# Attention beside a projection: TensorE in emission order, the scores and value products of two heads in turn in bursts, q, k and biases requested first

## The chip, the cores and the metric

The kernel runs on one core of a Trainium2 chip. The metric is the device time of one execution in microseconds, and lower is better. A core has a matrix engine (TensorE, PE in the profile; its weight loads are PEld), two engines for elementwise work (VectorE, DVE; ScalarE, ACT), GpSimd (POOL), and SyncE (SP), which in this kernel issues all DMA transfers from one queue. Each engine works through its own queue in order; semaphores tie the queues together.

## The reference

One layer over 512 tokens of width 1024. Branch A is a bidirectional Mamba-2 scan whose result `y` (2048 wide) goes through `w_proj_ssd`. Branch B is attention in three groups of 4 heads of width 64, with dilation 1, 4 and 16 and a window of half-width 64; the j-th heads of the three groups are combined by their softmax denominators.

```
for gi, (window, dilation) in enumerate(((128, 1), (512, 4), (2048, 16))):
    scores = einsum(q, k) / 8 - slope * dist          # window of |rel| <= 64 steps
    m = max(scores); p = exp(scores - m); den = sum(p)
    o = einsum(p, v) / den;  lse = m + log(den)
w = softmax(lse over the three groups);  y_att = sum(w * o) @ w_proj_attn
mix = (gate_a * (y_ssd @ w_proj_ssd) + gate_b * y_att) @ w_out
h = layer_norm(alpha * x + mix)
out = layer_norm(alpha * h + relu(h @ w_up)^2 @ w_down)
```

## The kernel before, in words

The stages follow each other on one TensorE: v and dt, the combined input projection interleaved with the scan (to 493.9 us), the attention interleaved with the first 12 of 16 pieces of the projection of `y` (`proj_a`, PSUM tiles `ps_pa`), then the last four pieces with the projection of the attention (`proj_b`, `ps_pb`), the output projection (`ps_o`), a layer norm, and the two MLP products.

The large products are float32 split in two halves of a reduced format (`mm3`, three matmuls a step, 512 columns each, lines 125 to 127). Each weight piece of 512 KB is loaded to `wraw` (line 87, three buffers), cast by ScalarE to `wh` (line 104) and subtracted by VectorE to `wl` (line 105), two buffers of each. A piece of `proj_a` is 24 matmuls.

The attention works on two heads at a time (`hh`), which lie in partitions 0 to 63 and 64 to 127 of the `q` and `k` tiles, so that a score matmul has 64 rows. In the trace each float32 matmul of the attention leaves two records. *Near* means dilation 1: scores at line 581 (192 or 256 columns), then VectorE adds the bias (589), takes the maximum (590) and negates it (592), and ScalarE takes the exponential (593). *Class* means dilations 4 and 16 (`gg`): scores at line 609, four matmuls of 128 columns a head, with lines 613 to 619 behind them. Then come the weights of the three groups (lines 624 to 641, tile `wg`); the near weights go through DRAM (`dr_w0`, lines 642 to 644) and back. `class_t` and `near_t` scale the probabilities and transpose them on TensorE (`ps_pt`, line 659; `ps_pn`, line 683), ScalarE copies them out, `class_v` (line 670, `ps_ac`) and `near_v` (line 698, `ps_an`) multiply by the values. A value product has 64 output partitions, the lower half for one head and the upper for the other, in one PSUM tile; near blocks b = 0 and b = 3 have one product of 64 rows and one of 128. `merge` adds near and class results and splits them into `ath` and `atl`, which `proj_b` reads.

`run` takes turns between the generators `attention()` and `proj_bg` by the amounts that they yield. In this stretch the order on every engine is then set by the scheduler of the program, which may move instructions ahead of others that wait; the same `run` around the scan stands in `tc.manual_schedule(engines={PE})`, which keeps TensorE in the order written. `ps_tile("tp", ..., 3)` and `ps_tile("y", ..., 2)` are PSUM tiles of one bank with 3 and 2 buffers. The pool `ap` holds the attention's tiles in memory that the scan's tiles had before (`reuse_waits`): a DMA into it waits until the old tile there has been read for the last time.

Of the kernel before, what the change touches and what calls it, by code (L numbers as in the profile page):

```python
# [10 lines left out]
F32 = mybir.dt.float32  # L11
# [5 lines left out]
P = 128  # L17
# [18 lines left out]
PACE = 0.6  # L36
# [8 lines left out]
def hybrid_layer_kernel(ctx: ExitStack, tc: tile.TileContext, t: dict, out: bass.AP):  # L45
# [504 lines left out]
    def attention():  # L550
        b0 = ap.tile([P, 4, 256], F32, name="b0")
        b12 = ap.tile([P, 8, P], F32, name="b12")
        dma.dma_start(b0, t["bias0"])
        dma.dma_start(b12, t["bias12"])
        v0 = ap.tile([P, 5, 256], F32, name="v0")
        vc = ap.tile([P, 4, 512], F32, name="vc")
        dma.dma_start(vc, dr_v.rearrange("(i r) d -> i r d", r=4)[:, :, 0:512])
        dma.dma_start(v0[:, 1:4, :], dr_v[64:448, 512:768].rearrange("(c p) d -> p c d", p=P))
        dma.dma_start(v0[0:64, 0, :], dr_v[0:64, 512:768])
        dma.dma_start(v0[0:64, 4, :], dr_v[448:512, 512:768])  # L560
# [6 lines left out]
        kr = [(max(0, P * b - 64), min(S, P * b + 192)) for b in range(NCH)]  # L567
        for i in range(2):
            qf = ap.tile([P, S], F32, name=f"q{i}", tag="q", bufs=2)
            kf = ap.tile([P, S], F32, name=f"k{i}", tag="k", bufs=2)  # L570
            dma.dma_start(qf, dr_qk[i])
            dma.dma_start(kf, dr_qk[6 + i])
            for bp in range(2):
                pss = [ps_tile("tp", f"ps_s0_{i}{bp}{hh}", 3) for hh in range(2)]
# [7 lines left out]
                for hh in range(2):  # L582
# [12 lines left out]
                    yield 2.0  # L595
        dma.dma_start(dr_st.rearrange("(b p) m -> p b m", p=P), st0.rearrange("p b a j -> p b (a j)"))
        for gg in range(2):
            for i in range(2):
                tl = 2 + gg * 2 + i
                qf = ap.tile([P, S], F32, name=f"q{tl}", tag="q", bufs=2)  # L600
                kf = ap.tile([P, S], F32, name=f"k{tl}", tag="k", bufs=2)
                dma.dma_start(qf, dr_qk[tl])
                dma.dma_start(kf, dr_qk[6 + tl])
                pss = [ps_tile("tp", f"ps_s{tl}_{hh}", 3) for hh in range(2)]
# [5 lines left out]
                for hh in range(2):  # L610
# [10 lines left out]
                    yield 2.0  # L621
# [23 lines left out]
        yield 1.0  # L645
# [3 lines left out]
        def tt_tile(name):  # L649
            nt[0] += 1  # L650
            return ap.tile([P, 4, P], F32, name=name, tag="qk"[nt[0] % 2], bufs=2)
# [12 lines left out]
        def class_v(i, hh, ptt):  # L664
            pr = slice(hh * HD, (hh + 1) * HD)
            if hh == 0:
                pcl[i] = ps_tile("y", f"ps_ac{i}", 2)
            for r in range(4):
                for gg in range(2):
                    pe.matmul(pcl[i][pr, r * P:(r + 1) * P], vc[:, r, (gg * 2 + i) * P + hh * HD:(gg * 2 + i) * P + (hh + 1) * HD], ptt[gg][:, r, :], start=(gg == 0), stop=(gg == 1))  # L670
# [20 lines left out]
        def near_v(i, b, tt):  # L691
            if b == 0:
                pn[i] = ps_tile("y", f"ps_an{i}", 2)
            for hh in range(2):
                pr = slice(hh * HD, (hh + 1) * HD)
                for q, (c0, c1, ck) in enumerate(cuts[b]):
                    n = c1 - c0
                    pe.matmul(pn[i][pr, b * P:(b + 1) * P], v0[:n, ck, (2 * i + hh) * HD:(2 * i + hh + 1) * HD], tt[:n, q * 2 + hh, :], start=(q == 0), stop=(q == 1))

        def merge(i):  # L700
            ac = ap.tile([P, S], F32, name=f"ac{i}", tag="vf", bufs=2)
# [5 lines left out]
        todo = []  # L707
        for i in range(2):
            for hh in range(2):
                a = class_t(i, hh, 0)  # L710
                yield 1.0
                b = class_t(i, hh, 1)
                yield 1.0
                for f in todo:
                    f()
                todo = [lambda i=i, hh=hh, a=a, b=b: class_v(i, hh, (a, b))]
# [298 lines left out]
```

## Time and profile before

| | |
|---|---|
| time, median of 3 runs (lowest, highest) | 1045.51 us (1044.17, 1045.84) |
| time of the profiled execution | 1044.5 us |
| its span, first to last instruction | 1042.7 us |
| TensorE busy | 1031.5 us, 99% |
| VectorE, ScalarE, GpSimd busy | 62%, 49%, 7% |
| first `ps_pa`, first `ps_pb` | 493.86 us, 608.3 us |
| output projection | 635.5 to 681 us |

Times inside the span are counted from the first instruction. A busy TensorE is one with a matmul in flight: since matmuls overlap, the step from one start to the next tells what one costs, and not its duration.

### The profile page before, as it was taken

Reading aid. Unit: us, or ns where it says so; the run is one execution under the profiler, and the core shown is the slowest. Engines: PE = TensorE matmul, PEld = TensorE weight load, DVE = VectorE, ACT = ScalarE, POOL = GpSimd, SP = SyncE. Lnnn points to the kernel's source line nnn. Section 1 sums busy time; section 2 is a strip of 40 time slices with the busy share of each in tenths; the row PEclk is TensorE's granted clock in tenths of the full one; section 3 lists DMA queues with packets and bytes.
Section 4 is the critical chain, followed back from the end, with each engine's and each line's share of the span. In section 5 each row is a group of like instructions: output and inputs, shape, how many; then the busy total and the mean of one; then the engine's idle time right before and its main releaser. Section 6 shows DMA issues by size and latency. Waiting matters only on the chain.

```text
span 1042.7 us, 13698 instructions
## 1 busy us (share of the span) xinstructions
PE 1031.5 (99%) x5169; PEld 852.9 (82%) x5169; DVE 648.6 (62%) x1009; ACT 511.6 (49%) x1009; POOL 74.1 (7%) x66
## 2 busy tenths in 40 slices
PE   9999999999999999999999999999999999999997
PEld 7888888888888888888777788798888888888886
DVE  4387988689979987784874356754442334443346
ACT  4444877478758865885564323213432113342120
POOL 0000101220221122021000000000000000000000
PEclk9999999999999999999999999999999999999999
DMA  6444354425543553655741358412333333333322
GB/s 233 153 156 126 130 186 159 141 92 177 187 132 118 186 185 118 201 183 172 253 124 51 111 154 292 129 41 59 88 97 101 101 94 91 99 102 101 89 93 80
DMA packets 48305, 140.42 MB, mean 135 GB/s; under 512 B 6512, under 2 KB 7280, under 8 KB 47984
## 3 DMA queue, kind: packets, MB, share of 16 engines
q1 hardware_dynamic: 48240, 139.56, 42.2%
q8 instruction: 40, 0.66, 0.3%
q14 instruction: 25, 0.20, 0.1%
HBM read 128.25 MB, written 11.30 MB: 134 GB/s over the span
## 4 chain that ended last, share of the span: by engine, by line
PE 94%; DVE 2%; DMA 1%; ACT 1%; issue 1%; POOL 0%; DVEq 0%; SPq 0%; ACTq 0%; POOLq 0%
PE ps_u L126 6%; PE ps_u L125 6%; PE ps_u L127 6%; PE ps_d L125 6%; PE ps_d L127 6%; PE ps_d L126 6%; PE ps_g L125 3%; PE ps_x L125 3%; PE ps_pa L125 3%; PE ps_g L127 3%; PE ps_g L126 3%; PE ps_x L126 3%; PE ps_x L127 3%; PE ps_pa L126 3%; PE ps_z L125 3%; PE ps_z L126 3%
## 5 line engine op out<-in xcount | busy, mean ns | idle before, releaser
L105 DVE TENSOR_TENSOR wl<-wraw,wh 128x1024 fp32r<-128x1024 f32 (+1 forms) x166 | 202.7, 1223 | 248.8 <-ACT wh L104 244.2
L104 ACT CAST wh<-wraw 128x1024 fp32r<-128x1024 f32 (+1 forms) x166 | 172.4, 1040 | 286.2 <-PE ps_d L127 108.6
L126 PE MATMUL ps_u<-htl,wh 128*128 128x512 f32 (+1 forms) x288 | 105.1, 366 | 0.3 <-DVE htl L857 0.3
L127 PE MATMUL ps_u<-hth,wl 128*128 128x512 f32 (+1 forms) x288 | 105.1, 365 | 0.0
L125 PE MATMUL ps_u<-hth,wh 128*128 128x512 f32 (+1 forms) x288 | 104.5, 366 | 0.3 <-ACT hth L856 0.2
L126 PE MATMUL ps_d<-wl,fh 128*128 128x512 f32 (+1 forms) x272 | 102.5, 377 | 0.0
L125 PE MATMUL ps_d<-wh,fh 128*128 128x512 f32 (+1 forms) x272 | 102.4, 377 | 0.0
L127 PE MATMUL ps_d<-wh,fl 128*128 128x512 f32 (+1 forms) x272 | 102.4, 377 | 0.0
L126 PEld LDWEIGHTS ps_u<-htl,wh 128*128 128x128 f32 x288 | 54.3, 189 | 9.3 <-DVE htl L857 0.5
L127 PEld LDWEIGHTS ps_u<-hth,wl 128*128 128x128 f32 x288 | 54.3, 189 | 8.8
L125 PEld LDWEIGHTS ps_u<-hth,wh 128*128 128x128 f32 x288 | 53.9, 188 | 9.3 <-ACT hth L856 0.7
L127 PEld LDWEIGHTS ps_d<-wh,fl 128*128 128x128 f32 x272 | 51.2, 188 | 9.5
L125 PEld LDWEIGHTS ps_d<-wh,fh 128*128 128x128 f32 x272 | 51.2, 188 | 9.4
L126 PEld LDWEIGHTS ps_d<-wl,fh 128*128 128x128 f32 x272 | 51.2, 188 | 9.4
L442 DVE SCALAR_TENSOR_TENSOR U<-bc,acr,U 128x128 f32<-128x128 f32 x128 | 47.5, 406 | 7.3 <-ACT U L440 7.1
L125 PE MATMUL ps_g<-xh,wh 128*128 128x512 f32 x128 | 51.5, 402 | 0.0
L125 PE MATMUL ps_pa<-yh,wh 128*128 128x512 f32 x128 | 51.0, 400 | 0.0
L125 PE MATMUL ps_z<-xh,wh 128*128 128x512 f32 x128 | 50.9, 398 | 0.0
L125 PE MATMUL ps_x<-xh,wh 128*128 128x512 f32 x128 | 50.9, 398 | 0.0
L126 PE MATMUL ps_pa<-yl,wh 128*128 128x512 f32 x128 | 50.5, 396 | 0.0
L127 PE MATMUL ps_pa<-yh,wl 128*128 128x512 f32 x128 | 50.0, 392 | 0.0
L127 PE MATMUL ps_x<-xh,wl 128*128 128x512 f32 x128 | 49.9, 390 | 0.0
(257 smaller groups left out, 2216.5 us busy)
## 6 DMA issues: line engine op xcount, KB each, us to landing
wraw<-in_w_in_dram SPq DMA_DIRECT2D x68, 512.0 KB, 3.6
bc<-dr_acr SPq DMA_DIRECT2D x32, 512.0 KB, 4.0
wraw<-in_w_up_dram SPq DMA_DIRECT2D x32, 512.0 KB, 3.6
wraw<-in_w_dn_dram SPq DMA_DIRECT2D x32, 512.0 KB, 3.6
be<-dr_ear SPq DMA_DIRECT2D x32, 256.0 KB, 4.4
wraw<-in_w_ps_dram SPq DMA_DIRECT2D x16, 512.0 KB, 3.9
dr_gate<-g SPq DMA_DIRECT2D x16, 256.0 KB, 2.0
wraw<-in_w_out_dram SPq DMA_DIRECT2D x8, 512.0 KB, 3.9
```

The lines of the kernel that those rows point to most:

```text
L104: act.copy(h[:, :width], r[:, :width])
L105: dve.tensor_sub(l[:, :width], r[:, :width], f32(h[:, :width]))
L125: pe.matmul(ps, lh, rh, start=(first and i == 0), stop=False)
L126: pe.matmul(ps, lh, rl, start=False, stop=False)
L127: ins = pe.matmul(ps, ll, rh, start=False, stop=(last and i == n - 1))
L442: dve.scalar_tensor_tensor(U[:, ch(c)], bcs[0][:, hh, ch(c)], acr[:, c, h:h + 1], U[:, ch(c)], op0=ALU.subtract, op1=ALU.min)
```

## The change

It has three parts. TensorE is kept in emission order around the `run` of attention and `proj_a`, and `proj_a` becomes a generator that yields after each 6 matmuls, so that the amounts yielded set where the attention's matmuls stand. The matmuls of the two heads stand in one burst in turn: near scores in four bursts, class scores in four, class value products in two, near value products with the head as the inner loop. And the queue's order changes: q and k of the first pair of heads, a bias and the next pair come first, the values after the near scores; the tiles for the values are allocated first, which moves the q, k and bias tiles to other addresses.

```diff
     def attention():
+        vc = ap.tile([P, 4, 512], F32, name="vc")
+        acs = [ap.tile([P, S], F32, name=f"ac{i}", tag="vf", bufs=2) for i in range(2)]
+        v0 = ap.tile([P, 5, 256], F32, name="v0")
+        load_qk(0)
         b0 = ap.tile([P, 4, 256], F32, name="b0")
+        dma.dma_start(b0, t["bias0"])
+        load_qk(1)
...
+        yield 4.0
+        def pair_tiles(n, name):
+            tag, bufs = (("tp", 3), ("y", 2))[n]
+            return [ps_tile(tag, f"{name}_{hh}", bufs) for hh in range(2)]
         for i in range(2):
             for bp in range(2):
-                pss = [ps_tile("tp", f"ps_s0_{i}{bp}{hh}", 3) for hh in range(2)]
+                pss = pair_tiles(bp, f"ps_s0_{i}{bp}")
...
-                    yield 2.0
+                yield 3.5
+        dma.dma_start(vc, dr_v.rearrange("(i r) d -> i r d", r=4)[:, :, 0:512])
...
-                    yield 2.0
+                yield 4.0
...
-        yield 1.0
+        yield 9.0
...
+        def class_v(i, ptt):
+            pcl[i] = ps_tile("y", f"ps_ac{i}", 2)
             for r in range(4):
                 for gg in range(2):
+                    for hh in range(2):
+                        v = vc[:, r, (gg * 2 + i) * P + hh * HD:(gg * 2 + i) * P + (hh + 1) * HD]
+                        pe.matmul(pcl[i][hh * HD:(hh + 1) * HD, r * P:(r + 1) * P], v, ptt[hh, gg][:, r, :], start=(gg == 0), stop=(gg == 1))
...
-            for hh in range(2):
-                for q, (c0, c1, ck) in enumerate(cuts[b]):
+            for q, (c0, c1, ck) in enumerate(cuts[b]):
+                for hh in range(2):
...
+        for k in range(0, 8, 2):
+            mm3(ps, [(wh[:, q * P:(q + 1) * P], wl[:, q * P:(q + 1) * P]) for q in (k, k + 1)], y_hl[i * 8 + k:i * 8 + k + 2], first=(i == 0 and k == 0), last=(i == 1 and k == 6))
+            if k < 6:
+                yield QT
...
-    run(attention(), proj_bg(a_order[:12]), 54.0, 62.4 * PACE)
+    with tc.manual_schedule(engines={mybir.EngineType.PE}):
+        run(attention(), proj_bg(a_order[:12]), 73.0, 48 * QT)
```

On TensorE, where the near scores begin (names before the arrow are the PSUM tile, behind it the operands; the last two digits of `ps_s0_000` are the block pair and the head). Before, from the last `ps_pa` ahead of the first score:

```order
L127 MATMUL ps_pa2_5039<-yh7_4775,wl78_4949 128x512
L581 MATMUL ps_s0_000_4853<-k0_4850,q0_4849 128x192
L581 MATMUL ps_s0_001_4854<-k0_4850,q0_4849 128x192
L581 MATMUL ps_s0_000_4853<-k0_4850,q0_4849 128x256
L581 MATMUL ps_s0_001_4854<-k0_4850,q0_4849 128x256
L581 MATMUL ps_s0_010_4920<-k0_4850,q0_4849 128x256
L581 MATMUL ps_s0_010_4920<-k0_4850,q0_4849 128x192
L125 MATMUL ps_pa3_4885<-yh8_4776,wh79_5035 128x512
L126 MATMUL ps_pa0_4885<-yl8_4808,wh79_5035 128x512
L127 MATMUL ps_pa0_4885<-yh8_4776,wl79_5036 128x512
L581 MATMUL ps_s0_011_4921<-k0_4850,q0_4849 128x256
L581 MATMUL ps_s0_011_4921<-k0_4850,q0_4849 128x192
```

Of the change, the second near burst with its neighbours:

```order
L124 MATMUL ps_pa1_4930<-yh1_4769,wh77_4869 128x512
L125 MATMUL ps_pa1_4930<-yl1_4787,wh77_4869 128x512
L126 MATMUL ps_pa1_4930<-yh1_4769,wl77_4870 128x512
L591 MATMUL ps_s0_01_0_4937<-k0_4842,q0_4841 128x256
L591 MATMUL ps_s0_01_1_4938<-k0_4842,q0_4841 128x256
L591 MATMUL ps_s0_01_0_4937<-k0_4842,q0_4841 128x192
L591 MATMUL ps_s0_01_1_4938<-k0_4842,q0_4841 128x192
L124 MATMUL ps_pa1_4930<-yh2_4770,wh77_4869 128x512
L125 MATMUL ps_pa1_4930<-yl2_4790,wh77_4869 128x512
L126 MATMUL ps_pa1_4930<-yh2_4770,wl77_4870 128x512
```

Before, the first score has 72 `ps_pa` matmuls ahead of it and only the first four scores change heads from one to the next; the rest stand in six small bursts with three `ps_pa` between them, one head in each after the first. Of the change, the first score has 18 `ps_pa` ahead of it, every burst holds two heads in turn, and 12 or 18 `ps_pa` stand between bursts; 54 stand between the last class scores and the first transpose.

On TensorE, the class value products of the first pair of heads (`tt0_0` is the transposed tile of `gg` 0 and head 0). Before, the end of the first head's burst, the near transposes and the start of the second head's:

```order
L670 MATMUL ps_ac0_5306<-tt0_0_5280,vc_4840 64x128
L670 MATMUL ps_ac0_5306<-tt1_0_5288,vc_4840 64x128
L683 MATMUL ps_pn0_0_5317<-tri_63,pt0_00_4859 64x128
L683 MATMUL ps_pn0_0_5317<-tri_63,pt0_00_4859 128x128
L683 MATMUL ps_pn0_0_5317<-tri_63,pt0_10_4910 64x128
L683 MATMUL ps_pn0_0_5317<-tri_63,pt0_10_4910 128x128
L670 MATMUL ps_ac0_5306<-tt0_1_5296,vc_4840 64x128
L670 MATMUL ps_ac0_5306<-tt1_1_5304,vc_4840 64x128
L670 MATMUL ps_ac0_5306<-tt0_1_5296,vc_4840 64x128
L670 MATMUL ps_ac0_5306<-tt1_1_5304,vc_4840 64x128
```

Of the change, the start of the one burst for both heads, with the `ps_pa` ahead of it:

```order
L124 MATMUL ps_pa4_5423<-yh3_4771,wh84_5344 128x512
L125 MATMUL ps_pa4_5423<-yl3_4793,wh84_5344 128x512
L126 MATMUL ps_pa4_5423<-yh3_4771,wl84_5345 128x512
L682 MATMUL ps_ac0_5436<-tt0_0_5360,vc_4837 64x128
L682 MATMUL ps_ac0_5436<-tt0_1_5388,vc_4837 64x128
L682 MATMUL ps_ac0_5436<-tt1_0_5374,vc_4837 64x128
L682 MATMUL ps_ac0_5436<-tt1_1_5405,vc_4837 64x128
L682 MATMUL ps_ac0_5436<-tt0_0_5360,vc_4837 64x128
```

The two bursts of eight matmuls, one a head, have become one of sixteen in which the head changes with every matmul, and the transposes that stood between them now follow it.

On SyncE, the requests from the last weight piece of this stretch before the attention's (`wraw80` is that piece). Before:

```order
L87 DMA wraw80_4946<-in_w_ps_dram 128x1024
L553 DMA b0_4835<-in_bias0_dram 128x1024
L554 DMA b12_4836<-in_bias12_dram 128x1024
L557 DMA vc_4840<-dr_v_72 128x4x512
L558 DMA v0_4839<-dr_v_72 128x3x256
L559 DMA v0_4839<-dr_v_72 64x256
L560 DMA v0_4839<-dr_v_72 64x256
L571 DMA q0_4849<-dr_qk_71 128x512
L572 DMA k0_4850<-dr_qk_71 128x512
L571 DMA q1_4977<-dr_qk_71 128x512
```

Of the change:

```order
L86 DMA wraw80_4924<-in_w_ps_dram 128x1024
L558 DMA q0_4841<-dr_qk_71 128x512
L559 DMA k0_4842<-dr_qk_71 128x512
L563 DMA b0_4845<-in_bias0_dram 128x1024
L558 DMA q1_4847<-dr_qk_71 128x512
L559 DMA k1_4848<-dr_qk_71 128x512
L566 DMA b12_4851<-in_bias12_dram 128x1024
L606 DMA vc_4837<-dr_v_72 128x4x512
L86 DMA wraw81_5007<-in_w_ps_dram 128x1024
L607 DMA v0_4840<-dr_v_72 128x3x256
L608 DMA v0_4840<-dr_v_72 64x256
```

The requests of `q0` and `k0` stood behind both biases and the four transfers of values, and now stand right behind `wraw80`; the values come behind the second bias, with a weight piece among them.

## Rows read from the trace of the kernel before

**Rows 1.** The page's opening: busy time of each engine with its share and instructions, TensorE's granted clock in 40 slices (tenths), and the chain that ended last by engine.

```profile
PE 1031.5 (99%) x5169; PEld 852.9 (82%) x5169; DVE 648.6 (62%) x1009; ACT 511.6 (49%) x1009; POOL 74.1 (7%) x66
...
PEclk9999999999999999999999999999999999999999
...
PE 94%; DVE 2%; DMA 1%; ACT 1%; issue 1%; POOL 0%; DVEq 0%; SPq 0%; ACTq 0%; POOLq 0%
```

**Rows 2.** Busy time in two stretches of 10 us of the attention: the stretch, its length, busy us and instructions of PE, PEld, DVE, ACT, POOL, the granted clock, the DMA engines' share and GB/s.

```profile
500.00:510.00 10.00, 10.00 (x46) 8.28 (x45) 7.21 (x10) 2.63 (x3) 0.00 (x0) 1.00 1.05 388
510.00:520.00 10.00, 9.85 (x45) 6.18 (x43) 8.42 (x34) 5.92 (x20) 0.00 (x0) 1.00 0.54 179
```

**Rows 3.** Three groups of the attention's matmuls by line and shape between 478 and 640 us: line, tiles, shape, count, busy us and mean ns of one (overlapped durations, not steps).

```profile
L609 PE MATMUL ps_s<-k,q 64*128 64x128 f32 x64 | 9.2, 285 | 0.0
L670 PE MATMUL ps_ac<-tt,vc 128*64 128x128 f32 x64 | 7.8, 276 | 0.0
L698 PE MATMUL ps_an<-tn,v 64*64 64x128 f32 x16 | 3.4, 294 | 0.0
```

**Rows 4.** TensorE in order of time in an undisturbed stretch of `ps_pa`: start, duration, line, tiles (first and last of 21 rows, one matmul each).

```profile
544.67 0.39 PE L125 MATMUL ps_pa<-yh,wh 128*128 128x512 f32 x1
...
549.20 0.39 PE L127 MATMUL ps_pa<-yh,wl 128*128 128x512 f32 x1
```

**Rows 5.** The score records alone in two stretches that split the first near burst (columns as in rows 2, without ACT and POOL; a count takes in records still running from before). The `ps_pa` behind the burst starts at the end of the second.

```profile
510.60:511.48 0.88, 0.86 (x8) 0.81 (x9) 0.00 (x0) 1.00 1.00 410
511.48:512.33 0.85, 0.85 (x6) 0.56 (x3) 0.00 (x0) 1.00 0.37 135
```

**Rows 6.** TensorE in order of time around the first class burst (4 matmuls of one head, 8 records).

```profile
522.37 0.40 PE L127 MATMUL ps_pa<-yh,wl 128*128 128x512 f32 x1
522.70 1.16 PE L609 MATMUL ps_s<-k,q 64*128 64x128 f32 x8
524.12 0.40 PE L126 MATMUL ps_pa<-yl,wh 128*128 128x512 f32 x1
```

**Rows 7.** TensorE in order of time in the value products of the first pair of heads, from two answers: a class burst of one head, the near block b = 0, and the block b = 1.

```profile
551.74 1.96 PE L670 MATMUL ps_ac<-tt,vc 128*64 128x128 f32 x16
553.63 0.63 PE L683 MATMUL ps_pn<-tri,pt 128*64 128x128 f32 x4
...
556.67 1.51 PE L698 MATMUL ps_an<-tn,v 64*64 64x128 f32 x8
558.11 0.33 PE L683 MATMUL ps_pn<-tri,pt 128*128 128x128 f32 x1
...
558.81 0.67 PE L698 MATMUL ps_an<-tn,v 128*64 128x128 f32 x8
559.40 0.52 PE L683 MATMUL ps_pn<-tri,pt 128*64 128x128 f32 x3
```

**Rows 8.** The DMA queue of SyncE in order of time, the nineteenth `ps_pa` on TensorE, DMA issues with KB each and median us to landing (of 496.5 to 503.3 us), and the time to landing of all loads of q and k.

```profile
496.56 0.33 SPq L87 DMA_DIRECT2D wraw<-in_w_ps_dram  x1
496.98 0.38 SPq L553 DMA_DIRECT2D b<-in_bias_dram  x1
...
500.59 0.61 SPq L571 DMA_DIRECT2D q<-dr_qk  x1
...
498.25 0.40 PE L127 MATMUL ps_pa<-yh,wl 128*128 128x512 f32 x1
...
b<-in_bias_dram SPq DMA_DIRECT2D x2, 512.0 KB, 5.1
...
wraw<-in_w_ps_dram SPq DMA_DIRECT2D x1, 512.0 KB, 3.7
...
DMA to landing us min/median/max: 2.6/3.3/8.0
```

**Rows 9.** VectorE in order of time over two blocks of near scores (line 589 add, 590 maximum).

```profile
520.48 0.41 DVE L589 TENSOR_TENSOR pt<-ps_s,b 128x256 f32<-128x256 f32 x1
...
520.87 0.34 DVE L589 TENSOR_TENSOR pt<-ps_s,b 128x192 f32<-128x192 f32 x1
521.13 0.66 DVE L590 TENSOR_REDUCE st<-pt 128x1 f32<-128x256 f32 x2
```

**Rows 10.** VectorE behind the last class scores (in brackets the idle time before and what ended it), and the first transpose of scaled probabilities on TensorE.

```profile
538.03 0.69 DVE L613 TENSOR_TENSOR pt<-ps_s,b 128x512 f32<-128x512 f32 x1 [1.60 <-PE ps_s L609]
...
545.55 0.69 DVE L738 SCALAR_TENSOR_TENSOR mixa<-ga,ps_pa 128x512 f32<-128x512 f32 x1 [2.88 <-PE ps_pa L127]
...
547.41 1.22 DVE L105 TENSOR_TENSOR wl<-wraw,wh 128x1024 fp32r<-128x1024 f32 x1
...
549.43 1.18 PE L659 MATMUL ps_pt<-tri,pt 128*128 128x128 f32 x8
```

**Rows 11.** Who waited for whom between 493 and 640 us: total us, times, longest.

```profile
DVE mixa L738 <- PE ps_pa L127: 16.1, 4, 8.5
```

**Rows 12.** TensorE's two longest waits in the output projection (in brackets the wait and what ended it).

```profile
652.22 0.51 PE L125 MATMUL ps_o<-wh,mixh 128*128 128x512 f32 x1 [0.23 <-ACT wh L104]
653.48 0.50 PE L126 MATMUL ps_o<-wl,mixh 128*128 128x512 f32 x1 [0.76 <-DVE wl L105]
```

**Rows 13.** The mean granted clock of the span (1 is full speed), and TensorE's longest wait of the whole execution, at its start.

```profile
core 0: 1042.7 us, clock 0.998
...
PE ps_warm L179 <- DVE warm L176: 1.2, 1, 1.2
```

More of the change, by code (lines that the diff above doesn't have):

```diff
@@ L550, in attention, with load_qk @@
     def attention():
+        vc = ap.tile([P, 4, 512], F32, name="vc")
+        acs = [ap.tile([P, S], F32, name=f"ac{i}", tag="vf", bufs=2) for i in range(2)]
+        v0 = ap.tile([P, 5, 256], F32, name="v0")
+        qk = {}
+        def load_qk(n):
+            qk[n] = [ap.tile([P, S], F32, name=f"{x}{n}", tag=x, bufs=2) for x in "qk"]
+            dma.dma_start(qk[n][0], dr_qk[n])
+            dma.dma_start(qk[n][1], dr_qk[6 + n])
+        load_qk(0)
         b0 = ap.tile([P, 4, 256], F32, name="b0")
+        dma.dma_start(b0, t["bias0"])
+        load_qk(1)
         b12 = ap.tile([P, 8, P], F32, name="b12")
-        dma.dma_start(b0, t["bias0"])
         dma.dma_start(b12, t["bias12"])
[L555 to L560, printed above, removed]
         st0 = ap.tile([P, NCH, 2, 4], F32, name="st0")
@@ L599, in attention @@
                 tl = 2 + gg * 2 + i
[L600 to L604, printed above, removed]
+                load_qk(tl)
+                qf, kf = qk[tl]
+                pss = pair_tiles(i, f"ps_s{tl}")
                 for r in range(4):
@@ L693, in near_v @@
                 pn[i] = ps_tile("y", f"ps_an{i}", 2)
-            for hh in range(2):
-                pr = slice(hh * HD, (hh + 1) * HD)
-                for q, (c0, c1, ck) in enumerate(cuts[b]):
+            for q, (c0, c1, ck) in enumerate(cuts[b]):
+                for hh in range(2):
+                    pr = slice(hh * HD, (hh + 1) * HD)
                     n = c1 - c0
                     pe.matmul(pn[i][pr, b * P:(b + 1) * P], v0[:n, ck, (2 * i + hh) * HD:(2 * i + hh + 1) * HD], tt[:n, q * 2 + hh, :], start=(q == 0), stop=(q == 1))
+            if b == NCH - 1:
+                merge(i)
         def merge(i):
-            ac = ap.tile([P, S], F32, name=f"ac{i}", tag="vf", bufs=2)
+            ac = acs[i]
             act.copy(ac.rearrange("p (i r) -> p i r", r=4), pcl[i].rearrange("p (r i) -> p i r", r=4))
@@ L707, in attention, with later @@
         todo = []
+        def later():
+            while todo:
+                todo.pop(0)()
         for i in range(2):
+            tts = {}
             for hh in range(2):
[L710 to L716, printed above, removed]
+                for gg in range(2):
+                    tts[hh, gg] = class_t(i, hh, gg)
+                    yield 1.4
+            later()
+            todo.append(lambda i=i, tts=tts: class_v(i, tts))
             for b in range(NCH):
                 tt = near_t(i, b)
-                yield 2.0
-                for f in todo:
-                    f()
-                todo = [lambda i=i, b=b, tt=tt: near_v(i, b, tt)]
-            todo.append(lambda i=i: merge(i))
-        for f in todo:
-            f()
+                yield 2.4
+                later()
+                todo.append(lambda i=i, b=b, tt=tt: near_v(i, b, tt))
+        later()
     ps_a = {}
@@ L733, in proj_a @@
         ps = ps_a[d]
-        mm3(ps, [(wh[:, k * P:(k + 1) * P], wl[:, k * P:(k + 1) * P]) for k in range(8)], y_hl[i * 8:i * 8 + 8], first=(i == 0), last=(i == 1))
+        for k in range(0, 8, 2):
+            mm3(ps, [(wh[:, q * P:(q + 1) * P], wl[:, q * P:(q + 1) * P]) for q in (k, k + 1)], y_hl[i * 8 + k:i * 8 + k + 2], first=(i == 0 and k == 0), last=(i == 1 and k == 6))
+            if k < 6:
+                yield QT
         if i == 1:
@@ L755, in proj_bg @@
         for d, i in order:
-            proj_a(d, i)
-            yield 5.2
-    run(attention(), proj_bg(a_order[:12]), 54.0, 62.4 * PACE)
+            yield from proj_a(d, i)
+    with tc.manual_schedule(engines={mybir.EngineType.PE}):
+        run(attention(), proj_bg(a_order[:12]), 73.0, 48 * QT)
     at_ctx.close()
@@ L767, in hybrid_layer_kernel @@
     for d, i, bs in ((6, 0, (0, 1)), (6, 1, (2, 3)), (7, 0, (4, 5)), (7, 1, (6, 7))):
-        proj_a(d, i)
+        for _ in proj_a(d, i):
+            pass
         for q in bs:
```

17 lines of the change are left out of this document (6 added, 11 removed).

## The prediction, as recorded before the changed kernel ran

> **What bounds the kernel now.** I read the page's opening first: TensorE is busy 99% of the span, the granted clock is at its upper level (2.4 GHz) in every slice, and 94% of the chain that ended last is TensorE [rows 1]. So time is gained where TensorE is given less work, and lost where it is made to wait. Then the stretches of the attention: TensorE is full there, but VectorE is at 7.2 and 8.4 us of 10, and between 500 and 510 us the DMA engines are full at 388 GB/s [rows 2]. TensorE doesn't feel either, because the scheduler lets it do 72 `ps_pa` before the first score. Last the steps of TensorE in order of time, as a busy row hides what a matmul costs: 20 steps of `ps_pa` take 4.53 us, 0.2265 each [rows 4].
>
> **TensorE's work, from the steps.** *Near scores.* The first near burst holds both kinds in one view: its first four matmuls change heads and give 8 records in 0.86 us, the last two are of one head and give 4 records in 0.85 us [rows 5]. Two heads, whose operands lie in different row halves, run side by side; less some 0.1 of leaving the burst (an estimate, a quarter of the 0.42 below), two matmuls of one head are 0.75, and four of two heads are 0.76 with 0.1 of entering, no more. In before only the first group of four is paired; three are not, and pairing each saves 0.75: 2.3 us.
>
> *Class scores.* One head's burst is 8 records between two `ps_pa`; the step from the `ps_pa` ahead to the second behind is 524.12 - 522.37 = 1.75 us, less two steps of 0.2265 that is 1.30 [rows 6]. A record of 128 columns costs 1.89 / 16 = 0.118 with the burst's end in it [rows 7], some 0.11 without, so 0.88 of the 1.30 is work and 0.42 entering and leaving. There are 64 records [rows 3], 7.0 us, all unpaired; paired they would be half. No row shows a pair of class scores. Bounds: nothing saved, and 3.5 us. I take 3.5, as the form (64 rows, two row halves, two PSUM banks) is that of the near scores, which differ only in columns [rows 5].
>
> *Bursts.* Before, the scores stand in 14 bursts (6 near, 8 class), of the change in 8. Six times 0.42 is 2.5 us. I take 2.4, since part of it may be in the terms above.
>
> *Class value products.* 16 records of one head take 1.89 us up to the next instruction [rows 7]. Near block 1, whose products are of the same form (128 rows, 64 columns, two column halves), gives 8 records of two heads in 0.59 us, the end included [rows 7], where eight of one head would take 0.94: half of 0.11 a record is 0.44, and 0.15 is left for the change of form. So a burst of two heads with 32 records takes about 1.89, as one head does now. Of four bursts, 64 records [rows 3], two are saved: 3.8 us. Bounds: 0.4 (only the two bursts' ends) and 4.0.
>
> *Near value products.* Block 0 alternates between 64 and 128 rows, and every change of form costs: 8 records in 1.44 us, against 0.59 in block 1 [rows 7]. With the head innermost, there are two groups instead of four and each holds both heads: half, 0.72. The same for block 3 and for the other pair of heads, 16 records of 64 rows in all [rows 3]: 4 x 0.72 = 2.9 us. Bounds: 1.2 if only the changes are saved (two of 0.15 each time), and 3.4 if a block costs 0.59.
>
> The sum is 2.3 + 3.5 + 2.4 + 3.8 + 2.9 = 14.9 us less work. `proj_a` in chunks adds nothing: the same matmuls in the same order, with stops on TensorE only where another burst is put in, and those are counted.
>
> **What the fixed order costs.** *The first scores.* Now 18 `ps_pa` stand ahead of them; the nineteenth starts at 498.25 us in before [rows 8], and there TensorE must stand until `q0`, `k0` have landed, with every `ps_pa` behind. `wraw80` is issued at 496.56 and takes 3.7, so it lands at 500.26; the first bias follows at 496.98 [rows 8]. In its place come `q0` and `k0`, issued at about 497.0 and 497.4. The engines are full, and 256 KB at 388 GB/s are 0.68 us [rows 2, 8], so they land at 500.9 and 501.6: 3.4 us of waiting. Bounds: a load of q or k takes 2.6 at the least [rows 8], 500.0 and 1.8 us; and if the pair lands as the first biases do, after 5.1 from 496.98 [rows 8], 502.1 and 3.8 us. I take 3.4. In before the same loads came out at 500.59 and TensorE had `ps_pa` to cover them; the cover is what the change takes away.
>
> *Later scores.* `q2` needs the buffers of `q0`, free after the second burst; it is wanted after 42 `ps_pa` and two bursts, 9.5 + 2.3 us. The closest are `q3` and `q5`: 30 `ps_pa` and a burst, 6.8 + 1.3 = 8 us, against a landing of 3.3 [rows 8]. Nothing.
>
> *The VectorE work of the scores.* Per near burst there are four tiles, two of 256 and two of 192 columns; two adds, 0.41 and 0.34, and two maxima, 0.66, are 1.4 us [rows 9], so 2.8 for four, and some more with the negations. Bursts are 12 to 18 `ps_pa` (2.7 to 4.1) and a burst of about 1.2 apart, 4 to 5.3 us, in which VectorE also makes its share of `wl`, 1.22 us [rows 10] for every 24 `ps_pa`, 0.6 to 0.9. It fits barely; the PSUM tiles of two bursts take up what slips. Nothing, but it is the narrowest place.
>
> *The weights.* From the add that the last class scores release to the first transpose of scaled probabilities the chain takes 549.43 - 538.03 = 11.4 us, of which 2.88 is VectorE waiting for a `ps_pa` that stands ahead in its queue [rows 10]. Of the change, the add and maximum of the other head come behind the last scores too, two operations of about 0.69 [rows 10]: 12.8 us with the wait, 9.9 without. The order puts 54 `ps_pa`, 12.2 us, between the last scores and the first transpose. Bounds: nothing and 0.6; I take nothing, as the wait needs a `ps_pa` that ends late. What is late would hold `ps_pt` and all `ps_pa` behind it.
>
> *After the attention.* `ps_o` waits 0.23 and 0.76 us for its weights [rows 12]. They run on a stream of loads, casts and subtractions that TensorE's use drives, so most of it moves along; an earlier TensorE meets it somewhat less ready. Bounds: nothing, and twice these waits more, 2.0 us. I take 0.5.
>
> The sum: -14.9 + 3.4 + 0.5 = -11.0 us. The profiled execution's 1044.5 us (1.8 outside the span) becomes 1033.5; the median of the runs shown is 1.0 higher, 1034.5. I predict 1034.0 us.
>
> **A rule weighed.** The idle time at the first scores is of a kind that the trace doesn't have: the longest wait of TensorE in it is 1.2 us, at the start [rows 13]. The Trainium skill, "TensorE: Matmul & The Clock Gate", section "Why this matters for your kernels", says that a longer gap between bursts sends TensorE back to half its clock. No run so far shows it here; what it would make of the time is the second rival.
>
> **The rivals.** *Pairing gives less than it should*, class scores or class value products alone: 3.5 or 3.4 us of the gain go, 1037.5 to 1038; both, 1041. Against it are the pairs of the near scores and of block 1 [rows 5, 7]. Chance 0.12.
>
> *The clock falls at the first scores.* TensorE stands 3.4 us and goes on at 1.2 GHz until it has been busy again. The one fall that the trace has is the start: a mean clock of 0.998 [rows 13] is 0.2% of 1042.7 us lost, 2.1 us. The same again gives 1034.0 + 2.1 = 1036. The trace has no wait of that length for it or against it. Chance 0.12.
>
> *The fixed order makes TensorE wait for VectorE*, the other side. `mixa` stands in VectorE's queue and waits for the end of a `ps_pa` piece, up to 8.5 us, 16.1 in four waits [rows 11]; what is queued behind it (the maximum of a near burst, the scaling of a transpose) is late, and now TensorE can't go on with `ps_pa` meanwhile. One such wait of 2.9 us [rows 10] ahead of the weights' chain gives 1037, two or three 1037 to 1041. It decides where the waits in the attention sum to 11 us more than the 3.4 taken: 1.4 at each of the eight score bursts. For it, VectorE at 8.4 of 10 [rows 2]. Against it, its queue is idle for 2.88 us inside the weights' chain [rows 10], which an order with other neighbours may give back. Chance of 2 to 8 us lost 0.12, of no gain or slower 0.08, half of that above 0.2%.
>
> *There is no stand at the first scores* (q and k land ahead of `wraw80`'s end, or TensorE comes later since `yl` is): 1031 to 1032. Chance 0.06.
>
> **How the numbers follow.** My case, 1032 to 1036.5 us, has 0.50. The unknown prices reach from 1029.5 (no wait, upper bounds of the value products) to 1041 (both pairings fail); the range of 1029.5 to 1040.5 us takes in all but the worst of the third rival and the end of the first, and leaves out some 0.12. A difference under 0.2%, about 2.1 us, can't be told from no change in this kernel. Faster by more than that has 0.92, within it 0.04, slower 0.04.
>
> **What would show it.** In the profile of the changed kernel: TensorE idle for 2 to 4 us ahead of the first score near 498 us, ended by the load of q or k; 8 bursts of scores, near ones of about 0.76 and class ones of about 0.9 us between their first and last record; two class value bursts of 1.9 us with 32 records; the first `ps_pb` near 597 instead of 608.3; the granted clock at its upper level behind the wait. I am wrong if the class scores keep 0.11 a record, if the clock in the slice after 500 us falls, or if TensorE's waits on VectorE's line 671 or the score tiles add up to more than 3 us.

## The result, and the profile after

The changed kernel takes 1036.08 us (median of 5, 1034.96 to 1039.81) against 1045.51 before; the ratio of the runs is 0.9916, 95% interval 0.9894 to 0.9937. Forecast were 1034.0 us, 1029.5 to 1040.5. The profiled execution took 1036.7 us, its span 1034.9 against 1042.7, and the first `ps_pb` comes at 600.0 instead of 608.3 us, where the prediction looked for 597. One execution of the third experiment's kernel, the profiled one, took 1109.1 us at a mean clock of 0.866 and is left out of its median and of the table of stages below.

The page's opening (compare [rows 1]): TensorE's busy share, the granted clock in slices, and the chain.

```profile
PE 1018.9 (98%) x5169; PEld 843.6 (82%) x5169; DVE 650.1 (63%) x1009; ACT 511.1 (49%) x1009; POOL 73.5 (7%) x66
...
PEclk9999999999999999999899999999999999999999
...
PE 89%; DMA 4%; DVE 4%; ACT 2%; issue 1%; SPq 0%; DVEq 0%; ACTq 0%
```

One slice of the clock is lower, and DMA's share of the chain has gone from 1% to 4%. TensorE's waits name the transfer (us in total, times, longest):

```profile
PE ps_s L591 <- DMA k<-dr_qk: 4.2, 1, 4.2
PE ps_warm L178 <- DVE warm L175: 1.2, 1, 1.2
...
PE ps_o L125 <- DVE wl L104: 0.8, 1, 0.8
PE ps_o L124 <- ACT wh L103: 0.7, 1, 0.7
```

TensorE in order of time there (start, duration, line, tiles):

```profile
498.21 0.40 PE L126 MATMUL ps_pa<-yh,wl 128*128 128x512 f32 x1
502.77 1.86 PE L591 MATMUL ps_s<-k,q 64*128 64x192 f32 x8 [4.16 <-DMA k<-dr_qk]
504.56 0.79 PE L124 MATMUL ps_pa<-yh,wh 128*128 128x512 f32 x1
...
506.86 0.63 PE L126 MATMUL ps_pa<-yh,wl 128*128 128x512 f32 x1
507.28 0.63 PE L124 MATMUL ps_pa<-yh,wh 128*128 128x512 f32 x1
...
509.59 1.03 PE L591 MATMUL ps_s<-k,q 64*128 64x256 f32 x8
```

And the same in stretches of 2 us (columns as in [rows 2]; the clock is the third number from the end):

```profile
500.00:502.00 2.00, 0.00 (x0) 0.00 (x0) 1.69 (x4) 0.32 (x1) 0.00 (x0) 1.00 0.95 316
502.00:504.00 2.00, 1.23 (x7) 1.17 (x8) 1.79 (x3) 0.00 (x0) 0.00 (x0) 0.56 1.02 359
504.00:506.00 2.00, 2.00 (x7) 1.16 (x4) 1.49 (x5) 0.00 (x0) 0.00 (x0) 0.50 1.02 410
506.00:508.00 2.00, 2.00 (x6) 1.61 (x5) 0.85 (x3) 0.86 (x1) 0.00 (x0) 0.50 0.98 382
508.00:510.00 2.00, 2.00 (x9) 1.32 (x10) 1.78 (x4) 0.63 (x3) 0.00 (x0) 0.73 0.05 20
```

TensorE stands for 4.2 us until `k0` has landed, then works at 0.50 of the clock (1.2 GHz) until about 509 us: a `ps_pa` step is 0.42 us (506.86 to 507.28) instead of 0.2265 [rows 4], and the first near burst takes 1.79 us to the next instruction, the second, at 2.4 GHz, 0.96.

The work that was to shrink did. The `ps_pa` behind the first class burst in before, which ends the burst of [rows 6]; then, of the change, a class burst, now of both heads, and the value products of the first pair of heads (compare [rows 7]):

```profile
523.78 0.50 PE L125 MATMUL ps_pa<-yh,wh 128*128 128x512 f32 x1
...
522.65 1.16 PE L621 MATMUL ps_s<-k,q 64*128 64x128 f32 x16
523.74 0.50 PE L124 MATMUL ps_pa<-yh,wh 128*128 128x512 f32 x1
...
560.17 1.97 PE L682 MATMUL ps_ac<-tt,vc 128*64 128x128 f32 x32
562.07 0.66 PE L695 MATMUL ps_pn<-tri,pt 128*128 128x128 f32 x4
...
565.39 0.81 PE L710 MATMUL ps_an<-tn,v 64*64 64x128 f32 x8
566.13 0.66 PE L695 MATMUL ps_pn<-tri,pt 128*128 128x128 f32 x4
```

16 class records in 1.09 us, where 8 took 1.08; 32 value records in 1.90, where 16 took 1.89; near block 0 in 0.74 instead of 1.44. Summing the steps between TensorE's records from the first `ps_pa` to the first `ps_pb`, by what each step begins with (a stand counts with the matmul ahead of it), in us:

| | before | changed | second experiment |
|---|---|---|---|
| `ps_pa`, 312 | 75.2 | 81.8 | 76.1 |
| scores, 96 | 15.1 | 9.0 | 8.2 |
| class value products, 64 | 7.6 | 3.8 | 3.8 |
| near value products, 64 | 8.2 | 5.2 | 5.1 |
| transposes, 64 | 8.4 | 6.4 | 6.2 |
| sum | 114.5 | 106.2 | 99.4 |

Behind the first `ps_pb` nothing changed but 0.5 us more in the output projection (46.25 instead of 45.75), and from its end on the two are alike within 0.01 us.

### The profile page after: what moved, and what is told of

The parts are those of the page before. It is cut to its first block, busy times and chain, and to the rows that moved or that the text cites. A ratio compares the mean times of both kernels' runs of the same rounds, so it can differ in the third digit from the quotient of the medians.

```text
span 1034.9 us, 13695 instructions
## 1 busy us (share of the span) xinstructions
PE 1018.9 (98%) x5169; PEld 843.6 (82%) x5169; DVE 650.1 (63%) x1009; ACT 511.1 (49%) x1009; POOL 73.5 (7%) x66
## 4 chain that ended last, share of the span: by engine, by line
PE 89%; DMA 4%; DVE 4%; ACT 2%; issue 1%; SPq 0%; DVEq 0%; ACTq 0%
PE ps_u L125 6%; PE ps_u L124 6%; PE ps_d L124 6%; PE ps_u L126 6%; PE ps_d L125 6%; PE ps_d L126 6%; PE ps_z L124 3%; PE ps_z L125 3%; PE ps_z L126 3%; PE ps_g L124 3%; PE ps_g L125 3%; PE ps_g L126 3%; PE ps_x L124 2%; PE ps_x L126 2%; PE ps_x L125 2%; PE ps_pa L124 2%
## 5 line engine op out<-in xcount | busy, mean ns | idle before, releaser
L103 ACT CAST wh<-wraw 128x1024 fp32r<-128x1024 f32 (+1 forms) x166 | 172.2, 1040 | 261.0 <-PE ps_d L126 108.6
L124 PE MATMUL ps_pa<-yh,wh 128*128 128x512 f32 x128 | 53.1, 415 | 0.0
```

Source lines behind the costliest of these rows:

```text
L103: act.copy(h[:, :width], r[:, :width])
L124: pe.matmul(ps, lh, rh, start=(first and i == 0), stop=False)
```

## The experiments

Ten kernels ran, two of them twice, in three sets, each beside the kernel before on the same chip. The median of the kernel before was 1045.1 to 1046.1 us in the three sets; the change itself ran only beside the 1045.5. Medians of different sets therefore compare to about 1 us, and the ratios are the better measure. "Stage" is from the first `ps_pa` to the first `ps_pb` in the profiled execution, "stand" TensorE's wait at the first scores. With the emission order alone the first scores come ahead of every `ps_pa`, so that its stage can't be compared.

| kernel | us, median | ratio to before, 95% interval | stage | stand |
|---|---|---|---|---|
| the change | 1036.08 | 0.9894 to 0.9937 | 106.2 | 4.2 |
| 1, stand filled | 1036.19 | 0.9896 to 0.9925 | 103.1 | none |
| 1 again | 1035.54 | 0.9895 to 0.9923 | 103.1 | none |
| 2, scores after 42 `ps_pa` | 1030.96 | 0.9850 to 0.9884 | 99.4 | none |
| after 30 `ps_pa` | 1031.85 | 0.9868 to 0.9904 | 99.4 | none |
| 3, no emission order | 1032.23 | 0.9850 to 0.9881 | | |
| 3 again | 1031.09 | 0.9854 to 0.9882 | 99.2 | 0.4 |
| 4, class scores head by head | 1040.79 | 0.9939 to 0.9965 | 108.5 | 4.3 |
| 8, class values head by head | 1038.03 | 0.9906 to 0.9938 | 107.1 | 3.7 |
| near values in the old loops | 1039.20 | 0.9930 to 0.9958 | 108.5 | 3.9 |
| 5, the second with later weights | 1030.62 | 0.9827 to 0.9861 | 99.4 | none |
| 6, old request order | 1042.80 | 0.9957 to 0.9981 | 112.4 | 10.6 |
| 7, emission order alone | 1067.14 | 1.0179 to 1.0230 | | 16.1 |

**What the stand costs: filled, and filled again.**

```diff
                 pss = pair_tiles(bp, f"ps_s0_{i}{bp}")
+                if i == 0 and bp == 0:
+                    for _ in range(18):
+                        pe.matmul(pss[0], yh[0][:, :P], yh[0], start=True, stop=True)
```

> The changed kernel, with 18 matmuls of 512 columns (the first y tile by itself, results overwritten) put on TensorE between the 18 ps_pa and the first near scores. They are extra work that fills the 4.2 us in which TensorE stands there; 18 x 0.2267 = 4.1 us. The wait for k0 is as long as before. Theory (the stand also costs the clock): the granted clock stays at its upper level, and the 6.1 us at 1.2 GHz behind the wait, worth 3.0 us, come back: 1036.1 - 3.0 = 1033 us, mean clock 0.998. Rival (the lower clock has another cause, or what it costs is hidden because VectorE or the weights are late anyway): the clock rises and the time stays at 1036, or neither changes.

> The first experiment's kernel once more (18 filler matmuls in the stand). Its profiled execution took 1033.3 us at a clock of 0.998, the others 1035.0 to 1038.4. Theory (the stand's clock is repaired in all, and the others lost it at the two waits of the output projection, 0.82 and 0.76 us in the profile, where the fourth experiment with 0.88 and 0.76 went to 1.2 GHz for 3 us): a profile of a longer execution shows 1.00 from 500 to 510 us and a lower clock around 640 us. Rival (k0 lands later in them, and a stand is left behind the filler): a wait of 1 us or more ahead of the first scores.

The filler does no useful work; it only takes the place of the stand. The clock is whole in the stage in both profiles, and the stage is 3.06 us shorter: that is the price of the lower clock inside the stage. The whole kernel gained no more than the intervals can tell (0.9910 and 0.9909 of the kernel before, the change 0.9916), so that in time the rival's 1036 us came. The first profile's stretch, and from the second profile, of an execution of 1035.6 us, one place where the gain can go (the output projection, TensorE in order of time, then stretches of the same kernel):

```profile
500.00:510.00 10.00, 10.00 (x52) 7.48 (x51) 9.48 (x25) 3.19 (x9) 0.00 (x0) 1.00 0.86 309
...
641.76 0.50 PE L124 MATMUL ps_o<-wh,mixh 128*128 128x512 f32 x1 [1.24 <-ACT wh L103]
643.02 0.50 PE L125 MATMUL ps_o<-wl,mixh 128*128 128x512 f32 x1 [0.76 <-DVE wl L104]
...
500.00:510.00 10.00, 10.00 (x51) 7.49 (x50) 9.38 (x25) 3.12 (x9) 0.00 (x0) 1.00 0.86 323
...
644.00:646.00 2.00, 2.00 (x6) 1.51 (x6) 1.19 (x1) 0.92 (x1) 0.00 (x0) 0.50 0.71 207
```

Two waits for weights with one matmul between them were followed by the lower clock, and the output projection took 48.3 us instead of the first profile's 46.3. That isn't the whole answer: four executions without a profile had a mean clock of 0.998, as the first profile's had, and took 1035.4 to 1038.4 us, where it took 1033.3. What held those up is in no trace and stays open. There was no stand behind the filler in either profile, so the rival of a later `k0` is out for these two executions, and for no other.

**The scores later.** The edit of the second experiment, and of the one with 30 `ps_pa` (6.8 and 75.8):

```diff
-        yield 4.0
+        yield 10.3
...
-        run(attention(), proj_bg(a_order[:12]), 73.0, 48 * QT)
+        run(attention(), proj_bg(a_order[:12]), 79.3, 48 * QT)
```

> The changed kernel with the first yield 10.3 instead of 4.0 (and 79.3 instead of 73.0 in run), so that 42 instead of 18 ps_pa stand ahead of the first scores, which come to about 503.7 us, after k0 has landed at 502.7; between later bursts 6 ps_pa fewer stand in some places, and 48 instead of 54 ahead of the first transpose. Theory (wait and clock are all that was lost): 4.2 + 3.0 us come back, 1029 us, no wait of over 0.5 us at the scores, clock 0.998. Rival (the chain from the scores to the weights is the next to be late): the first transpose waits, up to 5.4 us, and the time is 1031 to 1036. In the first run of this call (filler matmuls) only the 3.0 would come.

> The changed kernel with the first yield 6.8 instead of 4.0 (75.8 instead of 73.0 in run): 30 instead of 18 ps_pa ahead of the first scores, so that TensorE comes there at about 501.1 and the wait for k0, at 502.7, shrinks from 4.2 to some 1.5 us without going away. Theory (a short stand costs its length, a long one the clock too): the clock stays at 1.00 behind it and the time is 1036.1 - 2.7 - 3.0 = 1030.4 us. Rival (any stand at this place brings the clock down): 1036.1 - 2.7 = 1033.4 us with 6 us at 0.50.

Wait and clock go together, and 6.8 us of the stage with them; the first transpose doesn't wait. A stretch of the second experiment, and its TensorE's waits:

```profile
500.00:510.00 10.00, 10.00 (x52) 7.45 (x51) 9.69 (x22) 3.71 (x8) 0.00 (x0) 1.00 0.95 354
...
PE ps_o L125 <- DVE wl L104: 0.8, 1, 0.8
PE ps_o L124 <- ACT wh L103: 0.5, 1, 0.5
```

The median came 5.1 us below the change's, 2 us short of the theory; the profiled execution (1030.3) 6.4. It beats both kernels. With 30 `ps_pa` there was no short stand to be seen: the scores began at 501.70, as `k0` had landed 4.0 us after its request, where the change's took 5.3 (issues of k with KB and us to landing: of the change, of this kernel, and of the third experiment's kernel run again):

```profile
k<-dr_qk SPq DMA_DIRECT2D x1, 256.0 KB, 5.3
...
k<-dr_qk SPq DMA_DIRECT2D x1, 256.0 KB, 4.0
...
k<-dr_qk SPq DMA_DIRECT2D x1, 256.0 KB, 5.0
```

In the change the 1 MB of `vc` is requested at 499.84, while `k0` is on its way; here only at 503.47, behind a weight piece. That can't be the whole difference: in the third kernel run again it is requested at 503.89, after `k0` has landed, and `k0` took 5.0 us; in the first filled profile it is requested at 499.62, and `k0` took 4.6. What goes with the landing is the weight piece ahead in the queue: `k0` landed 1.2 to 1.3 us behind it in eight of the ten profiles with these requests, and 2.2 us behind it in the change and in the fourth experiment. Why it is later in those two stays open. What a stand of 1.5 us does to the clock has no single answer in the runs: with the emission order alone, below, a wait of 1.43 us had 0.50 behind it (529 to 531 us), and two of 1.50 and 1.64 us left 1.00. One of 0.4 us, below, left it at 1.00 too.

**Without the emission order.**

```diff
-    with tc.manual_schedule(engines={mybir.EngineType.PE}):
+    if True:
         run(attention(), proj_bg(a_order[:12]), 73.0, 48 * QT)
```

> The changed kernel without the emission order on TensorE: bursts, yields and requests as in the change, but the scheduler may move TensorE's instructions. It puts 34 ps_pa and then the first two near bursts as one; the rest stands as in the change. Theory (the fixed order costs the wait and the clock, and the gain is from the bursts and yields): TensorE reaches the first scores at about 502, waits under 1 us, clock 0.998, and the time is 1036.1 - 3.3 - 3.0 = 1030 us. Rival (the fixed order is what brings the gain): 1036 or more, towards 1045.

> The third experiment's kernel once more (no emission order on TensorE), for its profile in an undisturbed execution; the undisturbed times were 1029.6 to 1032.4. Theory: TensorE meets the first scores after 34 ps_pa at about 502 us, waits under 1 us, and the clock stays at 1.00; 1031 us. Rival (the scheduler's order takes its gain from other places): a wait as in the change, made up for elsewhere.

From the repetition's profile, the wait at the scores and two stretches, the second in the output projection behind two short waits for weights:

```profile
PE ps_s L591 <- DMA k<-dr_qk: 0.4, 1, 0.4
...
500.00:510.00 10.00, 9.56 (x54) 7.27 (x53) 9.75 (x24) 4.31 (x10) 0.00 (x0) 1.00 1.01 361
...
640.00:650.00 10.00, 10.00 (x39) 8.08 (x38) 4.90 (x4) 4.82 (x5) 0.00 (x0) 0.83 0.74 223
```

The scheduler puts 34 `ps_pa` ahead of the scores, which is enough, and the kernel is as fast as the second experiment. The emission order is not what brings the gain; it cost the stand.

**The emission order alone**, put around `run` in the kernel before with no other edit:

> The kernel before with nothing changed but the emission order on TensorE; its generators then put the first scores ahead of every ps_pa. Theory (the fixed order by itself costs, and it is the yields and requests that make it pay): TensorE stands from 493.9 to about 510 us, 16 us, and the clock falls; bursts hold two heads there too, which gives back some 8 us; later waits on VectorE between bursts without ps_pa add some: 1045.4 + 16 + 3 - 8 = 1056 us or more. Rival (the fixed order is what brings the gain): 1036 to 1045.

```profile
PE ps_s L581 <- DMA k<-dr_qk: 16.1, 1, 16.1
PE ps_pt L659 <- DVE pt L656: 4.5, 1, 4.5
PE ps_s L609 <- DVE pt L613: 3.1, 2, 1.6
...
PE ps_s L581 <- DVE pt L589: 1.4, 1, 1.4
```

2% slower. 16.1 us of stand, and 9 us of waits for VectorE (4.5 + 3.1 + 1.4) in which no `ps_pa` may pass: the third rival of the prediction exists, where the yields leave TensorE nothing between the bursts. The time is 11 us above the sum of the expectation, which had put no figure on these waits.

**The old request order.**

```diff
-        load_qk(0)
         b0 = ap.tile([P, 4, 256], F32, name="b0")
...
         dma.dma_start(b12, t["bias12"])
+        dma.dma_start(vc, dr_v.rearrange("(i r) d -> i r d", r=4)[:, :, 0:512])
...
+        load_qk(0)
+        load_qk(1)
```

> The changed kernel with the requests in the order of the kernel before: both biases, the four transfers of values, then q0, k0, q1, k1; order of TensorE and bursts as in the change. Theory (in the fixed order TensorE stands until k0 is there, wherever it is queued): k0 lands at about 510.5 instead of 502.7, the wait at the first scores is 12 instead of 4.2 us, the clock falls as it does in the change and for no longer: 1036.1 + 7.8 = 1044 us, so that the request order alone decides whether the whole change gains. Rival (the lower clock lasts with the wait): 1047 or more.

```profile
PE ps_s L595 <- DMA k<-dr_qk: 10.6, 1, 10.6
...
514.00:516.00 2.00, 2.00 (x6) 1.61 (x5) 1.18 (x6) 1.90 (x6) 0.00 (x0) 0.50 0.00 0
516.00:518.00 2.00, 2.00 (x13) 1.23 (x13) 1.02 (x2) 0.66 (x4) 0.00 (x0) 0.97 0.02 4
```

The wait is 6.4 us longer, the time 6.7, and the clock is back at 516 us, about 6 us behind the first score as in the change: the longer stand cost its length and no more clock. With the fixed order and 18 `ps_pa` ahead of the scores, the request order is worth most of what the change gained: without it the ratio is 0.9969 instead of 0.9916.

**Head by head: class scores, class values, near values.** The loop over the head was made the outer one in each in turn (the class scores' loops; the lines inside them only move):

```diff
-                for r in range(4):
...
-                    for hh in range(2):
...
+                for hh in range(2):
...
+                    for r in range(4):
...
```

> The changed kernel with the head as the outer loop in the class scores: the same four bursts, but four matmuls of one head and then four of the other. Theory of the prediction (a pair runs side by side when the head changes with every matmul): the four bursts take 1.9 instead of 1.1 us each, and the time is 1036.1 + 3.5 = 1039.5 us. Rival (it is enough that both heads stand in one burst, TensorE takes the second head's matmuls ahead): 1.1 us a burst and 1036 us, or something between.

> The changed kernel with the head as the outer loop in the class value products: one burst of sixteen matmuls, eight of one head and then eight of the other. Theory of the prediction (pairs only when the head changes with every matmul): the two bursts take 3.6 instead of 1.9 us each, 1036.1 + 3.4 = 1039.5 us. What the fourth experiment showed for the class scores (1.64 instead of 1.09 us, where nothing paired would be 2.0, so the second head's matmuls begin before the first head's are done): 2.5 to 3 us a burst, 1037.5 to 1038.

> The changed kernel with the loops of the near value products as in the kernel before (all products of one head, then of the other). Theory of the prediction: blocks 0 and 3 of both pairs of heads take 1.44 instead of 0.72 us, blocks 1 and 2 stay, 2.9 us more: 1039 us. Rival (TensorE takes the second head's products ahead, as it does in part in the fourth and eighth experiments): under 1 us more.

One burst of each (4, then class values, then near blocks 0 and 1):

```profile
523.12 1.71 PE L621 MATMUL ps_s<-k,q 64*128 64x128 f32 x16
524.76 0.50 PE L124 MATMUL ps_pa<-yh,wh 128*128 128x512 f32 x1
...
558.75 3.33 PE L682 MATMUL ps_ac<-tt,vc 128*64 128x128 f32 x32
562.01 0.66 PE L695 MATMUL ps_pn<-tri,pt 128*128 128x128 f32 x4
...
565.05 1.51 PE L710 MATMUL ps_an<-tn,v 64*64 64x128 f32 x8
566.50 0.66 PE L695 MATMUL ps_pn<-tri,pt 128*128 128x128 f32 x4
568.48 0.67 PE L710 MATMUL ps_an<-tn,v 128*64 128x128 f32 x8
569.07 0.66 PE L695 MATMUL ps_pn<-tri,pt 128*128 128x128 f32 x4
```

A class score burst takes 1.64 instead of 1.09 us (1.95 would be without pairs, an estimate at 0.11 a record and 0.2 for the change of form), a class value burst 3.26 instead of 1.90 (3.6 to 3.7 without, by the same estimate), near block 0 1.45 instead of 0.74, and block 1 0.59 in either order. So the order within the burst decides, but not all of it: some 0.3 to 0.4 us of the second head run beside the first wherever it follows in the same form. In a block of eight records that is everything, in a burst of 32 a fifth of what pairing saves. The stages grew by 2.3, 1.0 and 2.3 us; the value kernels' stands were 0.4 and 0.3 shorter and the clock was down for only some 3.3 us with class values head by head, so that by the steps of their own kind the three cost 2.2, 2.7 and 2.9 us. In median time they cost 4.7, 1.9 and 3.1, and by the ratios to the kernel before beside them 3.8, 0.6 and 2.9. The interval of the class values overlaps that of the change, so for them only the steps tell. With class scores head by head the profiled output projection lost 1.8 us more to a lower clock.

**Weights of the output projection later**, on top of the second experiment:

```diff
-        ws.add(t["w_up"][k], hold=("wu", k))
+        if k:
+            ws.add(t["w_up"][k - 1], hold=("wu", k - 1))
+    ws.add(t["w_up"][3], hold=("wu", 3))
...
-        wu.append(ws.get(1))
+        if k:
+            wu.append(ws.get(1))
...
+    wu.append(ws.get(1))
```

> The second experiment's kernel (42 ps_pa ahead of the first scores), and the four held pieces of w_up that are loaded in the first half of the output projection each one step later, behind the next pieces of w_out; same loads, other order. Theory: the two waits of TensorE there (0.51 and 0.76 us in that kernel; in the fourth experiment 0.88 and 0.76, behind which the clock stood at 1.2 GHz for 3 us) come from weight loads queued ahead of the piece that is wanted; they go, 1.3 us less, and with them the occasional fall of the clock: 1029 to 1029.5 us, and runs that differ less than the 4 us of that kernel. Rival (the DMA engines are simply full): the waits stay or move, 1031.

```profile
PE ps_o L124 <- DVE mb L769: 2.8, 1, 2.8
...
630.00:635.00 5.00, 5.00 (x21) 4.02 (x20) 3.61 (x4) 2.23 (x3) 0.00 (x0) 0.84 0.78 266
```

In the profiled execution, the slowest of five (1033.1 us, the others 1029.2 to 1030.8), the two waits for weights went, and a wait of 2.8 us for the gated projection (`mb`) came, with the lower clock behind it: there the rival holds, the waits moved. The median is 0.3 us below that of the second experiment, the intervals of the ratios overlap, and the executions differ by 3.9 us as they did there. So the expected gain of 1.3 us isn't shown, and whether the other executions had such a wait is in no trace.

## Why the prediction was right or wrong

The time fell inside the range, but by another case than the likeliest: the clock fell, as the second rival had it with 0.12, and that rival's figure was 1036 us. That it is met to 0.1 us is luck: the stand was 0.8 us longer and the clock 1.0 us dearer than the rival had them, the rival's 2.1 us were a misreading (below), the saved work was a little more, and the executions spread over 4.85 us. The time also lies in what the prediction called its own case, 1032 to 1036.5, but one of its signs of being wrong came true: the clock behind 500 us fell. Point by point:

*The work saved* came out near the sum's 14.9 us: 15.1 in the second experiment, which has neither a stand nor filler (99.4 against 114.5), and 15.5 in the filled kernel, whose stage without its filler (4.2) is 98.9. Its parts were less exact. Class values, 3.8, and near values, 3.0 for 2.9, were right. Scores with their bursts and the `ps_pa` steps around them gave some 6 to 7 instead of 8.2, and the transposes 2.0 that the sum didn't have: they wait and change form less often in the new order, which no experiment separated.

*The stand* was taken at 3.4 with bounds of 1.8 and 3.8, and was 4.2. The reckoning, two loads at the full rate behind the weight piece, puts `k0` some 1.4 us behind that piece, and in eight of the ten profiles with this request order it landed 1.2 to 1.3 behind it. In the change itself it was 2.2 (500.42 and 502.63 us), and these 0.8 us are what the term lacked; their cause is open.

*The step that failed is the price of the stand.* The sum put it at its length and left the clock to a rival with a chance of 0.12 and 2.1 us. The clock fell in every profile with a stand of 3.7 us or more, and behind two shorter single waits too (2.75 us with later weights, 1.43 with the emission order alone); in the change that cost 3.06 us of the stage. The rival's 2.1 us were read from the wrong place: the mean clock of 0.998 in the kernel before comes from the end of its span, where the last matmul begins at 1035.49 us and the granted clock is 0.58 from 1038 to 1040 and 0.50 after it; every stretch before that shows 1.00. That fall met no work of TensorE, so it has no price, and the first price of a fall in these runs is that of the filled kernel. (At the start the warm-up matmuls do stand 0.42 us apart, the step of 1.2 GHz, up to 3.7 us, but the clock view gives 1.00 there and the 2.1 us aren't theirs.) The rule cited from the Trainium skill ("TensorE: Matmul & The Clock Gate", section "Why this matters for your kernels") was weighed on the right place and then given too little: the trace agrees with it, 0.50 behind the stand. With this term the sum is -15.5 + 4.2 + 3.1 + 0.5 = -7.7 us, and the span fell by 7.8. The 15.5 and the 3.1 both come from the filled kernel's stage, so this says only that no large term is missing; with the second experiment's 15.1 the sum is -7.3.

*After the attention* 0.5 us were taken and 0.5 lost in the profiled execution; that the waits there can bring the clock down too was not foreseen.

*The fixed order* made nothing wait for VectorE: no wait at the weights or the later scores is in the profile, as forecast. The rival of the other side needs TensorE without `ps_pa` between bursts, as the order alone showed.

*What the fixed order is for* the prediction did not ask: it gave the order a price, and left open whether the bursts need it. The scheduler left the bursts together as well once they were written with these yields, and without the fixed order the kernel is faster.

## What to carry to other kernels

A fixed order on an engine turns every late transfer ahead of it into a stand of everything behind; put enough independent work ahead of the first instruction that needs the transfer (here 30 to 42 `ps_pa` instead of 18), and price a stand of several us on TensorE with the slower stretch behind it, not by its length alone. Matmuls that use half of the array should change halves with every matmul: in one burst but half after half, all but 0.3 to 0.4 us a burst of the gain is lost. A gain upstream can be lost in part in a later stage that waits for weights (0.5 us in the change, 2.0 us more in the second filled profile than in the first).

## What the runs showed of the hardware that was not expected

TensorE worked at 1.2 GHz for about 6 us behind a stand of 4.2 us and behind one of 10.6 us alike (0.97 in the stretch from 516 us on in the kernel with the old requests). In both the clock had fallen while TensorE still stood: 0.50 from 504 us on with the old requests, whose first score began at 510.30, and a mean of 0.63 from 502 to 503 us in the change. It can be less: with class values head by head, behind a stand of 3.7 us, the clock fell only about 1 us after work had begun again and was back some 3.3 us later.

Two short waits with a single matmul between them can also be followed by 1.2 GHz: 1.24 and 0.76 us were in the filled kernel's second profile, and 0.82 and 0.76 in the repetition of the third; 0.73 and 0.77 in the change were not. The lengths alone don't decide it: the filled kernel's first profile also had 0.82 and 0.76, the kernel with class values head by head had 0.90 and 0.76, and both kept 2.4 GHz. The lower clock there costs some 2 us (48.3 against 46.3 in the two filled profiles) and is one cause of the spread between executions of one kernel; the five of the change had mean clocks of 0.993 to 0.996. It isn't the only cause, as the filled kernel's executions of 1033.3 to 1038.4 us at 0.998 show.

The second head's products ran beside the first's without being next to them in the queue, for about four records (0.3 to 0.4 us, an estimate from the steps) in the class scores, the class values and near block 1. In near block 0, where the form changes between the products of one head, nothing of it was seen (1.45 us head by head, as before).
